# Seven block products for eight in the feed-forward networks, with weights split 1024 columns at a time

## The chip, the core and the metric

One NeuronCore of a Trainium2 chip runs the whole program. The metric is device time in microseconds (us). The kernel before takes 1405.89 us (median of 3 runs, 1405.14 to 1406.78). In what follows PE is TensorE, DVE is VectorE, ACT is ScalarE, POOL is GpSimd and SP is SyncE, which issues most of the transfers.

## The reference

A sequence of 256 rows of width 1024 goes through one block of a first model and two layers of a second. In all there are five feed-forward networks (one in the first block, two in each layer), and between them three mixing stages (attention and recurrence). Everything is float32. A feed-forward network, with `D_FF = 2816`, is

```python
def swiglu(h, w_gate, w_up, w_down):
    return (jax.nn.silu(h @ w_gate) * (h @ w_up)) @ w_down
```

with `h` the normalised rows, `w_gate` and `w_up` of 1024 x 2816 and `w_down` of 2816 x 1024. Around it stand the residual sum and the next norm. The mixing stages multiply by weights of the same height (1024) and do block attention, a gated recurrence or a differential attention on the result.

## The kernel before

**Tiles.** The 256 rows are two tiles `t` of 128. An operand of a matmul is split into a high part (rounded to the type that PE takes at full rate, `fp32r`) and a low part (the rest), and each product is three matmuls, high by high, high by low and low by high (`mm3`). The split of an operand is one copy on ACT (the high part) and one subtraction on DVE (the low part): `split`.

**Weights.** The host lays all weights out as 227 pieces of 128 x 2048 float32 (1 MB). SP loads them in order into three buffers `raw`, and `split_to` splits each piece into two halves of 1024 columns, 512 columns at a time (`SPLIT_W`), into the tiles `wh` (high) and `wl` (low), eight buffers of each (`W_BUFS`). `half` hands one half to the matmuls and splits four halves ahead (`SPLIT_AHEAD`). A half of a gate-and-up piece holds two K blocks of 128 rows by 512 columns; both row tiles use it, so it serves 12 matmuls of 512 columns.

**A feed-forward network** (`ffn_body`) goes over 11 blocks `j` of 256 hidden columns. `gu(t, j)` multiplies the rows of tile `t` by the 512 gate and up columns of block `j` (8 K blocks, 24 matmuls) and makes the hidden values: a Tanh on ACT, two operations on DVE (`th`, `hid`). `turn` transposes the hidden values on PE (4 transposes for both tiles) and splits them (`hh`, `hl`). `dn(t, j)` multiplies them by the 256 rows of `w_down` (12 matmuls) into two PSUM banks that stay open over all blocks. The order is gu(0,j), dn(0,j-1), gu(1,j), dn(1,j-1), so a block is 72 matmuls of 512 columns and 4 transposes.

**The order of work.** PE's order is that of the code (its schedule is manual); transposes and other short work are put into it by `Order`, which keeps a model of PE's time and lets a task go on after a wait written in the code (3.46 in `turn`). ACT, DVE and the transfers are ordered by the scheduler by priority, and `crit()` lifts the work on results over the splits. Each engine works its queue in order. A mixing stage ends with an output projection, for each tile both column halves, after which `boundary` transposes, scales and splits the rows for the next network.

After the sixth block (`j == 5`) some networks call `during`: the first block's network sets up parameters (`second_params`), and in each layer's first network `memory_prep` loads 256 rows of memory, transposes, scales (`uf`) and splits (`mh`, `ml`) them.

## Time and profile before

| | |
|---|---|
| median of 3 runs | 1405.89 us |
| the profiled execution: its own time | 1406.4 us |
| the profiled execution: span of the trace | 1404.6 us |
| busy share of PE, DVE, ACT, POOL | 99%, 66%, 54%, 4% |
| matmuls and transposes on PE | 6598 |
| weights and other data read from HBM | 244.37 MB, 175 GB/s over the span |
| clock granted to PE over the span | 0.999 |

How to read it: the span is cut by the trace into instructions with a start and a duration. Matmuls are pipelined, so the duration of one (about 390 ns) is longer than the distance from its start to the next one's start; it is this distance that counts for a sum. The same holds for DVE and ACT to a smaller degree: in a row of instructions each starts a little before the one ahead has ended. In the rows, `out<-in` names tiles as in the code, `x6` is six instructions, and what stands in brackets is the time that the engine sat idle before and what ended that wait.

### The profile page before, as it was taken

Reading aid. Unit: us, or ns where it says so; the run is one execution under the profiler, and the core shown is the slowest. Engines: PE = TensorE matmul, PEld = TensorE weight load, DVE = VectorE, ACT = ScalarE, POOL = GpSimd, SP = SyncE. Lnnn points to the kernel's source line nnn. Section 1 sums busy time; section 2 is a strip of 40 time slices with the busy share of each in tenths; the row PEclk is TensorE's granted clock in tenths of the full one; section 3 lists DMA queues with packets and bytes.
Section 4 is the critical chain, followed back from the end, with each engine's and each line's share of the span. In section 5 each row is a group of like instructions: output and inputs, shape, how many; then the busy total and the mean of one; then the engine's idle time right before and its main releaser. Section 6 shows DMA issues by size and latency. Waiting matters only on the chain.

```text
span 1404.6 us, 18011 instructions
## 1 busy us (share of the span) xinstructions
PE 1385.3 (99%) x6598; PEld 1126.6 (80%) x6598; DVE 922.8 (66%) x1789; ACT 763.6 (54%) x1527; POOL 58.2 (4%) x59
## 2 busy tenths in 40 slices
PE   8999999999999999999999999999999989999998
PEld 6777888888888888877888888888888767888887
DVE  7866587555585575768576665765756787755554
ACT  6556555444474454668565444644545568544442
POOL 0000000000010000022000000000000121000000
PEclk9999999999999999999999999999999999999999
DMA  8534546555446455454255555555454532455540
GB/s 291 174 122 158 180 142 237 192 191 189 180 157 233 180 180 180 168 197 161 91 183 191 195 187 194 207 191 197 164 206 155 182 120 94 172 188 194 192 180 30
DMA packets 37081, 246.59 MB, mean 176 GB/s; under 512 B 4736, under 2 KB 5760, under 8 KB 8064
## 3 DMA queue, kind: packets, MB, share of 16 engines
q1 hardware_dynamic: 35568, 243.09, 48.2%
q10 hardware_dynamic: 1424, 2.34, 0.5%
q8 instruction: 52, 0.85, 0.2%
q14 instruction: 37, 0.30, 0.1%
HBM read 244.37 MB, written 1.05 MB: 175 GB/s over the span
## 4 chain that ended last, share of the span: by engine, by line
PE 90%; DVE 6%; POOL 2%; ACT 1%; issue 1%; DMA 0%; SPq 0%; DVEq 0%; POOLq 0%; ACTq 0%
PE bank L149 86%; PE trbank L154 4%; POOL fac L261 2%; DVE wl L205 2%; DVE ms L953 1%; ACT p L454 1%; DVE nm L452 1%; DVE z L957 1%; DMA h<-in_x_dram 0%; DVE p L464 0%; DVE p L450 0%; DVE z L1015 0%; DVE p L1052 0%; DVE z L1017 0%; DVE z L1018 0%
## 5 line engine op out<-in xcount | busy, mean ns | idle before, releaser
L205 DVE TENSOR_TENSOR wl<-raw,wh 128x512 fp32r<-128x512 f32 x908 | 580.5, 686 | 194.4 <-ACT wh L204 187.6
L204 ACT CAST wh<-raw 128x512 fp32r<-128x512 f32 x908 | 513.0, 619 | 238.2 <-PE bank L149 227.9
L149 PE MATMUL bank<-wh,uh 128*128 128x512 f32 x1248 | 501.3, 402 | 0.0
L149 PE MATMUL bank<-wl,uh 128*128 128x512 f32 x1248 | 489.5, 392 | 0.0
L149 PE MATMUL bank<-wh,ul 128*128 128x512 f32 x1248 | 489.3, 392 | 0.0
L149 PEld LDWEIGHTS bank<-wh,ul 128*128 128x128 f32 x1248 | 234.6, 188 | 52.6
L149 PEld LDWEIGHTS bank<-wh,uh 128*128 128x128 f32 x1248 | 234.9, 188 | 48.8 <-issue 1.9
L149 PEld LDWEIGHTS bank<-wl,uh 128*128 128x128 f32 x1248 | 235.2, 188 | 46.1 <-DVE wl L205 0.3
L149 PE MATMUL bank<-wh,hh 128*128 128x512 f32 x440 | 172.8, 393 | 0.0
L149 PE MATMUL bank<-wl,hh 128*128 128x512 f32 x440 | 172.0, 391 | 0.0
L149 PE MATMUL bank<-wh,hl 128*128 128x512 f32 x440 | 172.0, 391 | 0.0
L355 ACT ACTIVATE th<-bank,rs 128x256 f32<-128x256 f32 x110 | 52.3, 475 | 179.2 <-PE bank L149 178.4
L356 DVE SCALAR_TENSOR_TENSOR th<-th,bank 128x256 f32<-128x256 f32 x110 | 46.3, 421 | 153.2 <-ACT th L355 153.2
L149 PEld LDWEIGHTS bank<-wl,hh 128*128 128x128 f32 x440 | 82.7, 188 | 18.0
L149 PEld LDWEIGHTS bank<-wh,hl 128*128 128x128 f32 x440 | 82.6, 188 | 17.9
L149 PEld LDWEIGHTS bank<-wh,hh 128*128 128x128 f32 x440 | 82.7, 188 | 17.6
L204 ACT CAST hh<-trbank 128x512 fp32r<-128x512 f32 (+1 forms) x60 | 33.1, 551 | 55.8 <-PE trbank L154 55.8
L261 POOL TENSOR_TENSOR r<-ms,mhalf 128x1 f32<-128x1 f32 x22 | 18.4, 838 | 909.5 <-DVE ms L271 909.5
L358 DVE SCALAR_TENSOR_TENSOR hid<-bank,rs,th 128x256 f32<-128x256 f32 x110 | 53.2, 484 | 3.6
L205 DVE TENSOR_TENSOR hl<-trbank,hh 128x512 fp32r<-128x512 f32 (+1 forms) x60 | 38.8, 646 | 16.5 <-ACT hh L204 13.5
L261 POOL TENSOR_TENSOR fac<-ms,mhalf 128x4 f32<-128x4 f32 (+2 forms) x26 | 38.4, 1477 | 246.8 <-DVE ms L954 139.3
L154 PEld LDWEIGHTS trbank<-cst,hid 128*128 128x128 f32 x220 | 27.6, 140 | 8.1
(223 smaller groups left out, 940.1 us busy)
## 6 DMA issues: line engine op xcount, KB each, us to landing
raw<-in_weights_dram SPq DMA_DIRECT2D x226, 1024.0 KB, 4.9
mem<-in_mem_dram ACTq DMA_DIRECT2D x4, 512.0 KB, 5.5
Tb<-in_rel_dram SPq DMA_DIRECT2D x3, 512.0 KB, 5.8
h<-in_x_dram SPq DMA_DIRECT2D x4, 256.0 KB, 3.8
raw<-in_weights_dram SPq DMA_DIRECT2D x2, 512.0 KB, 7.4
gf<-in_rows_dram SPq DMA_DIRECT2D x1, 512.0 KB, 4.1
out_dram<-h SPq DMA_DIRECT2D x2, 256.0 KB, 2.0
out_dram<-h SPq DMA_DIRECT2D x4, 128.0 KB, 1.8
```

Of the source, the lines that this page charges most:

```text
L149: pe.matmul(out=out, lhsT=lhsT, rhs=rhs, start=start, stop=stop)
L154: pe.transpose(out=out, in_=in_, identity=ident if identity is None else identity)
L204: act.copy(out=hi, in_=src)
L205: dve.tensor_tensor(out=lo, in0=src, in1=hi.bitcast(F32), op=ALU.subtract)
L261: pool.tensor_tensor(out=dst, in0=src, in1=mhalf[:, 0:n], op=ALU.pow)
L355: act.activation(out=th, in_=acc[:, 0:256], func=AF.Tanh, scale=rh[t])
L356: dve.scalar_tensor_tensor(out=th, in0=th, scalar=1.0, in1=acc[:, 0:256], op0=ALU.add, op1=ALU.mult)
L358: dve.scalar_tensor_tensor(out=hd, in0=acc[:, 256:512], scalar=r2[t], in1=th, op0=ALU.mult, op1=ALU.mult)
L452: dve.tensor_reduce(out=nm, in_=s, axis=AX.X, op=ALU.max, negate=True)
L454: act.activation(out=p[:, j, a, 0:n], in_=s[:, j], func=AF.Exp, bias=nm[:, j:j + 1], accum_out=sums[:, j, a:a + 1])
L953: dve.tensor_reduce(out=ms, in_=sq, axis=AX.X, op=ALU.add)
L957: dve.tensor_tensor(out=v, in0=v, in1=fac.unsqueeze(2).to_broadcast([128, n, w]), op=ALU.mult)
```

## The change

In each of the five networks the first seven blocks stay as they were, except that the order of a block is now gu(0,j), gu(1,j), dn(0,j-1), dn(1,j-1). The last four blocks are two groups of two blocks. A group multiplies the rows (2 tiles by 2 halves of K, each 128 x 512 values) by the weights of two blocks (2 halves of K by 2 blocks, each 512 x 512) by Strassen's scheme in the form with 7 products P1 to P7: seven products of 4 K blocks (12 matmuls) in place of eight. The sums of row operands are made once a network (`group_operands`), the sums of weights on DVE from the float32 pieces, 1024 columns at a time (`group_jobs`: `tn`, and in place in `raw` and `rawx`), and the products are joined on DVE (`joined`, tiles `jo`). Each product splits two halves of its own, and such a half serves 6 matmuls. The down products of two earlier blocks stand between the products.

The splits are 1024 columns wide, the buffers `wh` and `wl` are six each, the copies on ACT keep the order of the list of jobs (`in_order`), the output projections go by column half first and tile second, `during` is called after the seventh block, the last before the groups, and the memory rows have one buffer.

```diff
--- before.py
+++ after.py
...
-W_BUFS = 8
+W_BUFS = 6
...
-SPLIT_W = 512
+SPLIT_W = 1024
+GROUPS = 2
...
+    def plain(i):
+        for m in range(2):
+            add_job((i, m), i, lambda i=i, m=m: raws[i][:, 1024 * m:1024 * m + 1024])
...
+            if i in kept:
+                r = kept[i][0].tile([128, 2048], F32, tag="tx", bufs=2, name="rawx")
+            else:
+                r = wp.tile([128, 2048], F32, tag="raw", bufs=RAW_BUFS, name="raw")
...
+    def in_order(inst):
+        if order[0] is not None:
+            tc.add_manual_dep(inst.ins, order[0].ins.name,
+                              mybir.DependencyInfo(mybir.DependencyClass.NoSync, mybir.DependencyReason.DATA),
+                              reason="order of the operands")
+        order[0] = inst
...
+            key, piece, work = jobs[stream["split"]]
+            load_to(piece + 1 + LOAD_AHEAD)
+            r = work()
             hi = wp.tile([128, 1024], FR, tag="wh", bufs=W_BUFS, name="wh")
             lo = wp.tile([128, 1024], FR, tag="wl", bufs=W_BUFS, name="wl")
...
             for s in range(0, 1024, SPLIT_W):
-                split(hi[:, s:s + SPLIT_W], lo[:, s:s + SPLIT_W], r[:, 1024 * m + s:1024 * m + s + SPLIT_W])
-            parts[i, m] = (hi, lo)
+                in_order(split(hi[:, s:s + SPLIT_W], lo[:, s:s + SPLIT_W], r[:, s:s + SPLIT_W]))
+            parts[key] = (hi, lo)
...
-        split_to(2 * i + m + 1 + SPLIT_AHEAD)
+        split_to(at_job[i, m] + 1 + SPLIT_AHEAD)
...
+    def group_jobs(i, pool_, dn):
+        b11, b12, b22, b21 = i, i + 2, i + 3, i + 4
+        kept[b12] = kept[b22] = pool_
+        s = lambda m: slice(1024 * m, 1024 * m + 1024)
+        total = []
+        def job(name, piece, work):
+            for m in range(2):
+                add_job(((i, name), m), piece, lambda m=m: work(m))
+        def add(out, a, b):
+            dve.tensor_tensor(out=out, in0=a, in1=b, op=ALU.add)
+        def t2(m):
+            if m == 0:
+                total.append(pool_[0].tile([128, 2048], F32, tag="tn", bufs=1, name="tn"))
+            add(raws[b11][:, s(m)], raws[b11][:, s(m)], raws[b12][:, s(m)])
+            add(total[0][:, s(m)], raws[b11][:, s(m)], raws[b22][:, s(m)])
+            return total[0][:, s(m)]
+        def t3(m):
+            add(raws[b12][:, s(m)], raws[b12][:, s(m)], raws[b22][:, s(m)])
+            return raws[b12][:, s(m)]
+        def t4(m):
+            add(total[0][:, s(m)], total[0][:, s(m)], raws[b21][:, s(m)])
+            return total[0][:, s(m)]
+        job("P1", b11, lambda m: raws[b11][:, s(m)])
+        plain(dn[0])
+        job("P6", b22, t2)
+        job("P2", b21, lambda m: raws[b21][:, s(m)])
+        job("P5", b21, lambda m: raws[b11][:, s(m)])
+        plain(dn[1])
+        job("P7", b21, t3)
+        job("P3", b21, lambda m: raws[b22][:, s(m)])
+        job("P4", b21, t4)
...
+            full[id(u[2]), k0] = s
...
+        def element(t, j, acc):
+            hid_ready[t, j] = Ready()
             with crit():
                 th = fp.tile([128, 256], F32, tag="th", name="th")
                 act.activation(out=th, in_=acc[:, 0:256], func=AF.Tanh, scale=rh[t])
                 dve.scalar_tensor_tensor(out=th, in0=th, scalar=1.0, in1=acc[:, 0:256], op0=ALU.add, op1=ALU.mult)
-                hd = fp.tile([128, 256], F32, tag="hid", bufs=4, name="hid")
+                hd = fp.tile([128, 256], F32, tag="hid", bufs=5, name="hid")
                 dve.scalar_tensor_tensor(out=hd, in0=acc[:, 256:512], scalar=r2[t], in1=th, op0=ALU.mult, op1=ALU.mult)
-            hids[t] = hd
-            hid_ready[t, j] = ev
-            if j == NJ - 1:
-                side.spawn(turn((t,), j))
-            elif t == 1:
-                side.spawn(turn((0, 1), j))
+            hids[t, j] = hd
...
+        def group_operands():
+            x11, x12, x21, x22 = (full.pop((id(u[t][2]), k)) for t in range(2) for k in (0, 4))
+            sh = fp.tile([128, 4, 4, 128], FR, tag="sh", bufs=1, name="sh")
+            sl = fp.tile([128, 4, 4, 128], FR, tag="sl", bufs=1, name="sl")
+            dve.tensor_tensor(out=x22, in0=x21, in1=x22, op=ALU.subtract)
+            dve.tensor_tensor(out=x21, in0=x11, in1=x21, op=ALU.subtract)
+            dve.tensor_tensor(out=x11, in0=x22, in1=x11, op=ALU.subtract)
+            dve.tensor_tensor(out=x12, in0=x12, in1=x11, op=ALU.add)
+            for n, (name, x) in enumerate((("P6", x11), ("P5", x22), ("P7", x21), ("P3", x12))):
+                split(sh[:, n], sl[:, n], x)
+                S[name] = sh[:, n], sl[:, n]
+            for name, t, k in (("P1", 0, 0), ("P2", 0, 4), ("P4", 1, 4)):
+                S[name] = u[t][0][:, k:k + 4], u[t][1][:, k:k + 4]
...
+        def group(g):
+            j = n_conv + 2 * g
+            a, b = (j - 2, j - 1) if g == 0 else (j - 1, j - 2)
+            last = g == GROUPS - 1
+            i = plan["group", g]
+            def joined(x, y, op, into=None):
+                o = fp.tile([128, 512], F32, tag="jo", bufs=4, name="jo") if into is None else into
+                with crit():
+                    dve.tensor_tensor(out=o, in0=x, in1=y, op=op)
+                return o
+            def prod(name):
+                acc = bank()
+                xh, xl = S[name]
+                for k in range(4):
+                    wh, wl = half((i, name), k // 2, 512)
+                    mm3(acc, xh[:, k], xl[:, k], wh[:, k % 2], wl[:, k % 2], k == 0, k == 3)
+                return acc
+            c11 = fp.tile([128, 512], F32, tag="jo", bufs=4, name="jo")
+            p1_ = prod("P1")
+            with crit():
+                act.copy(out=c11, in_=p1_)
+            dn(1, a)
+            dn(0, a)
+            U = joined(prod("P6"), c11, ALU.add)
+            joined(prod("P2"), c11, ALU.add, c11)
+            element(0, j, c11)
+            if last:
+                side.spawn(turn((0,), j, 4.2))
+            V = joined(prod("P5"), U, ALU.subtract)
+            dn(0, b)
+            p7 = prod("P7")
+            element(1, j + 1, joined(V, p7, ALU.subtract))
+            joined(p7, U, ALU.add, U)
+            if last:
+                side.spawn(turn((1,), j + 1, 4.9))
+            dn(1, b)
+            joined(prod("P3"), V, ALU.add, V)
+            element(0, j + 1, V)
+            side.spawn(turn((0,) if last else (0, 1), j + 1, 4.2))
+            joined(prod("P4"), U, ALU.add, U)
+            element(1, j, U)
+            side.spawn(turn((1,) if last else (0, 1), j, 4.2))
...
+        for j in range(n_conv):
+            more = 1 <= j < n_conv - 1
             gu(0, j)
-            if j:
+            gu(1, j)
+            if more:
                 dn(0, j - 1)
-            gu(1, j)
-            if j:
                 dn(1, j - 1)
-            if during and j == 5:
+            if j == 0:
+                group_operands()
+            if during and j == n_conv - 1:
                 during()
-        j = NJ - 1
-        gu(0, j)
-        dn(0, j - 1)
-        gu(1, j)
-        dn(1, j - 1, (0,))
+        for g in range(GROUPS):
+            group(g)
+        j = NJ - 2
         dn(0, j)
+        dn(1, j + 1, (0,))
+        dn(0, j + 1, by_c=True)
         fin(0)
-        dn(1, j - 1, (1,))
-        dn(1, j)
+        dn(1, j + 1, (1,))
+        dn(1, j, by_c=True)
         fin(1)
...
-        for t in range(2):
-            for c in range(2):
+        for c in range(2):
+            for t in range(2):
                 acc = lin((get_oT(t)[0], get_oT(t)[1], o_ready[t]), (p1 + 2 * c, p1 + 2 * c + 1))
                 sl = h[t][:, 512 * c:512 * c + 512]
                 with crit():
                     dve.tensor_tensor(out=sl, in0=acc, in1=sl, op=ALU.add)
-            res[0].append(boundary(t, h[t], gcol(G_F2 + 8 * layer)))
-            res[1].append(row_rstd(h[t]))
+                if c:
+                    res[0].append(boundary(t, h[t], gcol(G_F2 + 8 * layer)))
+                    res[1].append(row_rstd(h[t]))
...
-            ms = mp.tile([128, 1024], F32, tag="mem", bufs=2, name="mem")
+            ms = mp.tile([128, 1024], F32, tag="mem", bufs=1, name="mem")
```

What the change moves is shown at two places on DVE. The first is the steady work of a network before: one block and a half, where `wl` are splits of weights, `th` and `hid` the hidden values, `hl` the split of the transposed hidden values.

```order
L356 SCALAR_TENSOR_TENSOR th<-th,bank 128x256
L358 SCALAR_TENSOR_TENSOR hid<-bank,rs,th 128x256
L205 TENSOR_TENSOR wl<-raw,wh 128x512 x6
L356 SCALAR_TENSOR_TENSOR th<-th,bank 128x256
L358 SCALAR_TENSOR_TENSOR hid<-bank,rs,th 128x256
L205 TENSOR_TENSOR wl<-raw,wh 128x512 x6
L205 TENSOR_TENSOR hl<-trbank,hh 128x512
```

Now, in the first network, where the first group ends and the second begins; `tn`, `raw` and `rawx` as outputs are sums of weights, `jo` joined products.

```order
L464 SCALAR_TENSOR_TENSOR th<-th,jo 128x256
L267 TENSOR_TENSOR raw<-raw,rawx 128x1024
L466 SCALAR_TENSOR_TENSOR hid<-jo,rs,th 128x256
L223 TENSOR_TENSOR hl<-trbank,hh 128x512
L267 TENSOR_TENSOR tn<-raw,rawx 128x1024
L223 TENSOR_TENSOR hl<-trbank,hh 128x512
L267 TENSOR_TENSOR raw<-raw,rawx 128x1024
L223 TENSOR_TENSOR wl<-tn,wh 128x1024
L267 TENSOR_TENSOR tn<-raw,rawx 128x1024
L267 TENSOR_TENSOR rawx<-rawx 128x1024 x2
L223 TENSOR_TENSOR wl<-tn,wh 128x1024
L223 TENSOR_TENSOR wl<-raw,wh 128x1024 x2
```

Six sums of 1024 columns have come between the splits of weights, and a split waits in DVE's queue behind the sums and joins ahead of it.

The second place is the memory rows of a layer's first network, on DVE; `uf` scales, `ml` is the split. Before they stand between the splits of ordinary blocks:

```order
L356 SCALAR_TENSOR_TENSOR th<-th,bank 128x256
L299 TENSOR_TENSOR uf<-trbank,gc 128x512
L358 SCALAR_TENSOR_TENSOR hid<-bank,rs,th 128x256
L205 TENSOR_TENSOR ml_4470<-uf,mh_4469 128x512
L299 TENSOR_TENSOR uf<-trbank,gc 128x512
L205 TENSOR_TENSOR ml_4470<-uf,mh_4469 128x512
L205 TENSOR_TENSOR wl<-raw,wh 128x512 x6
```

Now they stand inside the first group:

```order
L267 TENSOR_TENSOR rawx<-rawx 128x1024
L371 TENSOR_TENSOR uf<-trbank,gc 128x512
L267 TENSOR_TENSOR tn<-tn,raw 128x1024
L223 TENSOR_TENSOR wl<-raw,wh 128x1024
L223 TENSOR_TENSOR ml_4336<-uf,mh_4335 128x512
L371 TENSOR_TENSOR uf<-trbank,gc 128x512
L223 TENSOR_TENSOR wl<-raw,wh 128x1024
L556 TENSOR_TENSOR jo<-bank,jo 128x512
```

The four scalings and four splits of memory rows moved from blocks where DVE serves 72 matmuls with 12 short splits to a group where sums and joins stand beside them.

## Rows read from the trace of the kernel before

**Rows 1.** The page's busy times: us (share of the span), instructions of each engine.

```profile
PE 1385.3 (99%) x6598; PEld 1126.6 (80%) x6598; DVE 922.8 (66%) x1789; ACT 763.6 (54%) x1527; POOL 58.2 (4%) x59
```

**Rows 2.** Busy time by stretch: two networks, two mixing stages; then PE's clock.

```profile
core 0: us, PE busy (x) PEld busy (x) DVE busy (x) ACT busy (x) POOL busy (x), PEclk, DMA share, GB/s
212.00:400.00 188.00, 188.00 (x847) 153.47 (x846) 115.83 (x208) 93.52 (x172) 3.11 (x3) 1.00 0.54 194
400.00:587.00 187.00, 187.00 (x855) 153.93 (x854) 122.49 (x220) 99.92 (x185) 5.70 (x6) 1.00 0.52 187
587.00:710.00 123.00, 119.97 (x676) 96.00 (x675) 88.08 (x194) 85.51 (x206) 18.32 (x16) 1.00 0.41 145
1083.00:1213.00 130.00, 122.90 (x656) 97.13 (x656) 97.55 (x211) 86.77 (x211) 22.25 (x17) 0.99 0.36 123
```

**Rows 3.** Timeline of PE in a block: start, duration, instruction.

```profile
345.46 0.60 PE L154 MATMUL trbank<-cst,hid 128*128 128x128 f32 x4
345.82 0.48 PE L149 MATMUL bank<-wh,uh 128*128 128x512 f32 x1
...
346.60 0.39 PE L149 MATMUL bank<-wh,uh 128*128 128x512 f32 x1
...
349.34 0.39 PE L149 MATMUL bank<-wh,uh 128*128 128x512 f32 x1
...
350.03 0.40 PE L149 MATMUL bank<-wh,hh 128*128 128x512 f32 x1
...
352.13 0.40 PE L149 MATMUL bank<-wh,hh 128*128 128x512 f32 x1
```

**Rows 4.** Timeline of DVE in a block of the first network.

```profile
303.94 4.01 DVE L205 TENSOR_TENSOR wl<-raw,wh 128x512 fp32r<-128x512 f32 x6 [3.42 <-ACT wh L204]
307.88 0.42 DVE L356 SCALAR_TENSOR_TENSOR th<-th,bank 128x256 f32<-128x256 f32 x1
308.34 0.48 DVE L358 SCALAR_TENSOR_TENSOR hid<-bank,rs,th 128x256 f32<-128x256 f32 x1
308.74 3.69 DVE L205 TENSOR_TENSOR wl<-raw,wh 128x512 fp32r<-128x512 f32 x6
```

**Rows 5.** Groups of DVE by shape: count, busy us, mean ns, idle before.

```profile
L205 DVE TENSOR_TENSOR wl<-raw,wh 128x512 fp32r<-128x512 f32 x908 | 580.5, 686 | 194.4 <-ACT wh L204 187.6
L1269 DVE TENSOR_TENSOR h<-h,gf 128x1024 f32<-128x1024 f32 x2 | 2.4, 1219 | 0.0
L402 DVE SCALAR_TENSOR_TENSOR h<-bank,h 128x512 f32<-128x512 f32 x18 | 12.3, 687 | 2.2 <-PE bank L149 2.0
L205 DVE TENSOR_TENSOR hl<-trbank,hh 128x256 fp32r<-128x256 f32 x10 | 4.2, 419 | 3.3 <-ACT hh L204 3.3
L205 DVE TENSOR_TENSOR ml<-uf,mh 128x512 fp32r<-128x512 f32 x8 | 5.5, 692 | 2.1 <-ACT mh L204 2.0
```

**Rows 6.** Groups of ACT by shape.

```profile
L204 ACT CAST wh<-raw 128x512 fp32r<-128x512 f32 x908 | 513.0, 619 | 238.2 <-PE bank L149 227.9 <-DMA raw<-in_weights_dram 5.2 <-ACT wh L204 2.8
L355 ACT ACTIVATE th<-bank,rs 128x256 f32<-128x256 f32 x110 | 52.3, 475 | 179.2 <-PE bank L149 178.4 <-DVE hl L205 0.7
L267 ACT ACTIVATE junk<-h 128x1024 f32<-128x1024 f32 x18 | 19.0, 1058 | 24.7 <-DVE h L1197 19.8 <-DMA h<-in_x_dram 2.9 <-DVE h L402 1.5
```

**Rows 7.** The transfers of weights: KB each, median us from issue to landing.

```profile
raw<-in_weights_dram SPq DMA_DIRECT2D x226, 1024.0 KB, 4.9
```

**Rows 8.** Waits of PE: us in total, times, longest.

```profile
PE trbank L154 <- DVE z L1018: 3.3, 2, 2.3
PE trbank L154 <- DVE p L1052: 2.2, 1, 2.2
PE trbank L154 <- DVE o L957: 1.6, 3, 0.8
```

**Rows 9.** Timeline of PE in the last mixing stage; idle before in brackets.

```profile
1129.50 0.66 PE L154 MATMUL trbank<-cst,p 128*128 128x128 f32 x2 [2.18 <-DVE p L1052]
```

**Rows 10.** The stretch in which PE's clock fell (columns as in rows 2).

```profile
1128.90:1132.30 3.40, 2.80 (x8) 2.33 (x9) 3.40 (x8) 2.24 (x7) 0.00 (x0) 0.50 0.21 34
```

More of the change, by code (lines that the diff above doesn't have):

```diff
@@ L188, with add_job @@
     stream = {"load": 0, "split": 0}
-    raws, parts = {}, {}
+    raws, parts, kept = {}, {}, {}
     NP = weights.shape[0]
+    jobs, at_job = [], {}
+    piece_at = {}
+    def add_job(key, piece, work):
+        at_job[key] = len(jobs)
+        jobs.append((key, piece, work))
+    def plain(i):
+        for m in range(2):
+            add_job((i, m), i, lambda i=i, m=m: raws[i][:, 1024 * m:1024 * m + 1024])
     def load_to(n):
@@ L203, in split @@
     def split(hi, lo, src):
-        act.copy(out=hi, in_=src)
+        c = act.copy(out=hi, in_=src)
         dve.tensor_tensor(out=lo, in0=src, in1=hi.bitcast(F32), op=ALU.subtract)
+        return c
+    order = [None]
+    def in_order(inst):
[4 more added lines that the diff above has]
+        order[0] = inst
     def split_to(n):
-        while stream["split"] < min(n, 2 * NP):
-            i, m = divmod(stream["split"], 2)
-            load_to(i + 1 + LOAD_AHEAD)
-            r = raws[i]
+        while stream["split"] < min(n, len(jobs)):
+            key, piece, work = jobs[stream["split"]]
+            load_to(piece + 1 + LOAD_AHEAD)
+            r = work()
             hi = wp.tile([128, 1024], FR, tag="wh", bufs=W_BUFS, name="wh")
@@ L287, in new_u @@
         return uh, ul, []
+    full = {}
     def put_T(u, k0, n, src, gains=None, gain1=None, keep=None):
@@ L390, in dn @@
             hh, hl = hidT[t, j]
-            order = [(c, k) for c in range(2) for k in kts] if j == NJ - 1 else [(c, k) for k in kts for c in range(2)]
-            for c, k in order:
-                wh, wl = half(dnp(j), k, 512)
-                mm3(accd[t][c], hh[:, k], hl[:, k], wh[:, c], wl[:, c], j == 0 and k == 0, j == NJ - 1 and k == 1)
+            done[t] += len(kts)
+            order = [(c, k) for c in range(2) for k in kts] if by_c else [(c, k) for k in kts for c in range(2)]
+            for n, (c, k) in enumerate(order):
+                wh, wl = half(plan["dn", j], k, 512)
+                first = (t, c) not in started
+                started.add((t, c))
+                mm3(accd[t][c], hh[:, k], hl[:, k], wh[:, c], wl[:, c], first,
+                    done[t] == 2 * NJ and (c, k) == [o for o in order if o[0] == c][-1])
+        done = [0, 0]
         def fin(t):
@@ L407, in fin @@
                 finish(t)
-        for j in range(NJ - 1):
+        S = {}
+        def group_operands():
[11 more added lines that the diff above has]
+                S[name] = u[t][0][:, k:k + 4], u[t][1][:, k:k + 4]
@@ L422, in ffn_body @@
-        dn(1, j - 1, (0,))
+        for g in range(GROUPS):
+            group(g)
+        j = NJ - 2
         dn(0, j)
+        dn(1, j + 1, (0,))
+        dn(0, j + 1, by_c=True)
         fin(0)
-        dn(1, j - 1, (1,))
-        dn(1, j)
+        dn(1, j + 1, (1,))
+        dn(1, j, by_c=True)
         fin(1)
@@ L1191, in second_mix @@
         res = [[], []]
-        for t in range(2):
-            for c in range(2):
+        for c in range(2):
+            for t in range(2):
                 acc = lin((get_oT(t)[0], get_oT(t)[1], o_ready[t]), (p1 + 2 * c, p1 + 2 * c + 1))
@@ L1245, in memory_kv, with plan_ffn @@
             side.spawn(task())
-    P_FFN = 3 * NJ
+    plans = {}
+    for n in range(30):
+        plain(n)
+    p = 30
+    def plan_ffn():
+        nonlocal p
+        plans[p] = ffn_plan(p)
+        p += P_FFN
+    plan_ffn()
+    for layer in range(2):
+        plan_ffn()
+        for n in range(16):
+            plain(p + n)
+        p += 16
+        plan_ffn()
+    assert p == NP
     p = 0
```

88 lines of the change are left out of this document (64 added, 24 removed).

## The prediction

> **What bounds the kernel now.** I read the page's busy times first: PE is busy 1385.3 us of the span of 1404.6, and DVE 66% of it [rows 1]. The table by stretch says where PE is not busy: in the two networks that it shows PE is busy 188.00 of 188.00 and 187.00 of 187.00 us, and the idle time lies in the mixing stages, 3.0 us (123.00 less 119.97) and 7.1 us (130.00 less 122.90) [rows 2]. So a network costs what its matmuls cost, as long as DVE and ACT bring the split weights in time; DVE is busy 115.83 of the 188 us [rows 2]. The timeline gives the price of a matmul. From 346.60 to 349.34 us twelve matmuls on row operands start, 0.228 us each; from 350.03 to 352.13 nine on hidden values, 0.233 each; four transposes take 0.36, or 0.09 each [rows 3].
>
> **What the change removes.** A group has 7 x 12 = 84 product matmuls where two blocks had 4 x 24 = 96, and the 48 down matmuls stay. Ten groups save 120 matmuls, 120 x 0.228 = 27.4 us. All of it lay on the path, since PE never paused there.
>
> The Trainium skill's page "TensorE: Matmul & The Clock Gate", section "Back-to-back issue gap", puts a matmul of 512 columns in a stream with its weight loads at about 131 ns. By that the 120 would save 15.7 us and the sum below would end 12 us higher. The trace differs, with 228 ns from start to start [rows 3], so the sum goes by it and the rule gets no chance of its own.
>
> **What it adds on DVE.** First the prices. Six splits of 512 columns take 3.69 us and one takes 0.686, so they start 0.60 apart, 0.09 less than one lasts [rows 4, 5]. An operation on 1024 columns lasts 1.219 us [rows 5]; with the same overlap of 0.09 it occupies DVE for 1.13. No row shows 1024 columns back to back. The bounds are 1.22 (no overlap) and 1.07 (twice the 0.533 us by which 1024 exceeds 512, so without any fixed cost). I take 1.13, since the overlap is what rows 4 show. A join of a product in PSUM costs what a residual sum from PSUM does, 0.687, so 0.60 in a row [rows 5]. `th` and `hid` last 0.42 and 0.48 [rows 4], so 0.33 and 0.40 in a row, a 256-column `hl` 0.33 [rows 5]. The copy of 1024 columns on ACT lies between 0.619 for 512 columns and 1.058 for a Square of 1024 [rows 6]; I take 1.05.
>
> In an ordinary block this is no burden: 6 splits at 1.13 in place of 12 at 0.60 (6.8 for 7.2 us), with 72 matmuls and 4 transposes, 16.9 us, to hide under. In a group it is. There are 14 splits for products, 4 for down weights and 8 sums, 26 x 1.13 = 29.4 us, then 7 joins, 4 pairs of `th` and `hid` and the `hl`, 4.2 + 2.9 + 1.2: 37.7 us of DVE against 132 matmuls and 8 transposes, 31.1 us of PE. ACT has 18 x 1.05 + 4 x 0.475 and about 2 us of other copies, 23 us [rows 6], and stays under PE.
>
> What can be done ahead is limited by the six buffers. The first group profits: its first splits and sums run while gu(0,6) and gu(1,6) still multiply, and I price its waits at nothing (DVE has the last conventional block's idle time as cover; gone, the group would wait the 6.6 us of its excess). The second does not. Its splits stand in DVE's queue behind the last two splits of group one (P4), and the first of these needs the buffer of the first half of P7. From the end of that half of P7 I count both queues up to the second half of P4 in group two, which PE needs there.
>
> - PE: 168 matmuls (108 on rows, 60 on hidden values) and 12 transposes: 108 x 0.228 + 60 x 0.233 + 12 x 0.09 = 39.7 us.
> - DVE, by its order from the split of P4 to that second half: 20 splits and 8 sums of 1024 columns, 28 x 1.13 = 31.7; 10 joins, 6.0; 5 `th` and 5 `hid`, 3.7; 2 `hl` of 512 and 2 of 256 columns, 1.9: 43.3 us. Ahead of it stand the end of the matmul (0.39 less 0.23 [rows 3], 0.16) and the copy on ACT, 1.05, behind it the last split's own end, 0.09: 44.6 us.
>
> PE waits for the difference, 4.9 us a network, 24.5 us in five. With 1.07 it is 3.2, with 1.22 it is 7.4 a network: 16 to 37.
>
> **What stands behind it.** DVE is then still late. The two down splits that follow cost 1.5 and 2.1 us (each with a `th`, a `hid` or a join in front) while PE takes 1.37 and 1.40 for a half: 0.8 us. The last hidden tile passes a join, a Tanh (0.475 [rows 6]), `th`, `hid`, two transposes and a split on each engine, 3 us, but on DVE behind splits for the next network, and the first rows of the next network come from the same queue. PE has 8.4 us of down products to cover this. I take 2.0 us a network for all this, 10 us in five; bounds 0.8 and 4.
>
> - The memory rows add 8 operations of 0.60 [rows 5], 4.8 us, to group one of two networks. They lay in ordinary blocks; now DVE has about 2 us to spare ahead of P4. 3 us each, 6 us; bounds 0 and 9.6.
> - `group_operands` adds 4 sums and 4 subtractions of 512 columns, 4.8 us, in the first blocks, where DVE is idle 6.6 us a block ((188.00 less 115.83) / 11 [rows 2]). Its cover holds except where the new network's rows are late too: 1 us a network, 5 us; bounds 0 and 24.
> - Mixing stages: PE waits there for chains of short operations on DVE and ACT [rows 8]. A chain's operation can stand behind a split that lasts 1.22 in place of 0.69 on DVE and 1.05 in place of 0.62 on ACT. DVE is 75% busy there (97.55 of 130 [rows 2]), so a handover loses about 0.2 us (half of the 0.53 that the split lasts longer, in 75% of the cases); six waits with four handovers each in the last stage make 5 us, and I take nothing for the other two. The new order of the output projection also asks for the second tile's attention result 24 matmuls (5.5 us) earlier. I take these 5 us; bounds -3 (the new order also takes a split's wait away) and 14.
> - Transfers: a group loads 6 pieces in 31 us, a block 3 in 16.9. A piece lands 4.9 us after its issue [rows 7], and the buffers that it waits for come free more than 8 us of DVE work before it is needed: nothing; if one were late, up to 4.9 us a group.
>
> **Sum.** -27.4 + 24.5 + 10 + 6 + 5 + 5 = +23 us on the profiled execution's 1406.4, or 1429.5. The median shown is 0.5 us below that execution: 1429.
>
> **Rivals.**
>
> - The clock falls too, 1441 us. In the last mixing stage PE waited 2.18 us after light work [rows 9] and its clock was 0.50 of full, 1.2 GHz, for 3.4 us [rows 10], which cost half of them, 1.7 us. If the waits of each second group and two more in the last mixing stage do the same, 7 x 1.7 = 12 us come on top. Against it: another wait of 2.3 us [rows 8] stands in the same stage, whose mean clock of 0.99 [rows 2] is one fall's worth, and in a group dense matmuls lie between waits of 1 to 2 us. The skill's page "TensorE: Matmul & The Clock Gate", section "HAM oscillation", warns of just such kernels, in which pauses that recur bring the slow clock each time; rows 10 agree that it happens.
> - Faster, 1389 us: DVE keeps up. It is one mechanism: the queue of the second group fits under PE's 39.7 us. It decides at 0.96 us for an operation on 1024 columns (28 x 0.17 = 4.9 us less). Then the waits, the tail and the memory rows' price vanish, and -27.4 + 5 + 5 remain. For it speak DVE's 34% of idle time [rows 1] and its 194.4 us of waiting ahead of splits [rows 5]; against it the row of 1.219 us and that the buffers forbid using the idle time of other blocks.
> - In between, 1403 us: the wait of the second group comes as counted (24.5), but all the rest is hidden. The mixing stages would have to keep their waits, which are already there with shorter splits.
>
> That the saving does not come is not a rival: the order has 120 matmuls fewer on PE.
>
> **Chances.** The forecast 0.71, the slower clock 0.14, DVE keeping up 0.08, the case between 0.07. A measurement of this kernel tells about 0.2% (2.8 us) from no change. The case between falls on either side of that bound: 0.03 faster, 0.04 the same. So faster 0.11, the same 0.04, slower 0.85. The range goes from 1411, where the run costs 1.07 and the small terms half of theirs (-27.4 + 16 + 5 + 3 + 3 + 5, about +5), to 1446, where it costs 1.22 (+12) and the mixing stages 5 more.
>
> **What would show it.** Right: in the second group of each network PE's waits are on `wl`, DVE shows no gap for about 43 us there, its 1024-wide splits start 1.13 apart, the first group of the first network has no wait, and a network takes some 2 us longer than before (5 in the two with memory rows), not 5.5 shorter. Wrong: PE without waits in the groups, or splits of 1.0 us; PE waiting for transfers; a clock of 0.5 in the groups.

## The result, and the profile after

The changed kernel takes 1437.65 us (median of 4 runs, 1436.41 to 1437.94), the kernel before 1405.78 beside it: ratio 1.0224, with a 95% interval of 1.0207 to 1.0242. It is slower, by 31.9 us where 23 were forecast, and lies inside the range.

The page of the profiled execution (its own time 1436.41 us) answers to [rows 1] and [rows 5]: the span, busy time by engine, the head of the chain that ended last, and the split on DVE.

```profile
span 1434.6 us, 17202 instructions
PE 1376.8 (96%) x6478; PEld 1100.2 (77%) x6478; DVE 1106.8 (77%) x1590; ACT 797.0 (56%) x1168; POOL 65.3 (5%) x59
PE 72%; DVE 20%; ACT 3%; issue 2%; POOL 2%; DMA 1%; DVEq 0%; POOLq 0%; ACTq 0%
L223 DVE TENSOR_TENSOR wl<-raw,wh 128x1024 fp32r<-128x1024 f32 x434 | 526.0, 1221 | 134.2 <-ACT wh L222 125.7
```

PE has 120 matmuls and transposes fewer (6478 for 6598) and is busy 8.5 us less, but the span is 30.0 us longer, and a fifth of the chain now runs over DVE (6% before). A split of 1024 columns lasts 1.221 us, the 1.219 that the sum's price was made from.

Cut at the networks' first and last matmuls, the tables by stretch (columns as in [rows 2]) show where the 30 us are. First the kernel after: network 1, the gap behind it, network 2, the first and the last mixing stage between networks.

```profile
213.24:404.20 190.96, 186.23 (x829) 149.13 (x827) 154.81 (x188) 102.07 (x126) 3.22 (x2) 1.00 0.49 171
404.20:406.36 2.16, 0.17 (x1) 0.00 (x1) 2.12 (x6) 2.16 (x5) 0.00 (x0) 1.00 0.92 372
406.36:603.10 196.74, 190.20 (x845) 152.09 (x846) 160.89 (x206) 109.29 (x140) 4.84 (x5) 0.99 0.51 178
603.10:724.07 120.97, 116.30 (x653) 92.13 (x652) 82.92 (x156) 79.86 (x168) 19.30 (x16) 1.00 0.42 152
1110.36:1242.77 132.41, 120.69 (x635) 94.06 (x634) 93.50 (x174) 81.47 (x174) 22.75 (x17) 0.99 0.38 135
```

And the kernel before, networks 1 and 2 and the same two mixing stages.

```profile
212.65:402.18 189.53, 189.53 (x854) 154.67 (x853) 117.36 (x208) 95.25 (x176) 4.06 (x3) 1.00 0.53 191
402.18:591.81 189.63, 189.63 (x870) 156.22 (x868) 124.35 (x226) 102.18 (x190) 5.19 (x6) 1.00 0.53 189
591.81:710.47 118.66, 115.63 (x654) 92.36 (x653) 84.51 (x187) 81.52 (x199) 17.39 (x15) 1.00 0.41 144
1087.89:1214.02 126.13, 119.03 (x636) 93.92 (x634) 94.44 (x205) 82.72 (x204) 21.32 (x16) 0.99 0.36 123
```

The five networks, cut in this way, take +1.4, +7.1, +2.7, +6.2 and +1.3 us: 18.7 us more, where 27.4 us of matmuls are gone. The gap is new, 2.2 us; the two mixing stages are 2.3 and 6.3 us longer; the start is 0.6 longer. That is 30.1.

Inside the networks the table by stretch shows the first and the second group of network 1, then of network 2, where the memory rows are made.

```profile
321.69:352.78 31.09, 31.09 (x137) 25.18 (x136) 29.71 (x35) 20.59 (x23) 0.00 (x0) 1.00 0.55 203
352.78:389.56 36.78, 33.38 (x145) 25.52 (x144) 36.46 (x44) 20.62 (x26) 0.00 (x0) 1.00 0.33 114
516.24:549.30 33.06, 32.75 (x153) 26.66 (x152) 32.38 (x42) 21.49 (x28) 1.73 (x1) 1.00 0.61 205
549.30:588.46 39.16, 33.81 (x145) 25.50 (x144) 38.61 (x46) 21.13 (x28) 0.00 (x0) 1.00 0.31 105
```

The first group takes 31.09 us and PE never pauses. In the second DVE is busy 36.46 of 36.78 us and PE pauses: it is idle 3.4 us of the 5.7 by which this group is longer than the first; the rest the trace doesn't show as idle time. DVE's timeline there has the columns of [rows 4]; of the run from the split of P4 in group one to that in group two it shows the start, two operations in a row, and the end.

```profile
344.31 1.23 DVE L223 TENSOR_TENSOR wl<-tn,wh 128x1024 fp32r<-128x1024 f32 x1 [1.11 <-ACT wh L222]
...
360.45 1.22 DVE L223 TENSOR_TENSOR wl<-tn,wh 128x1024 fp32r<-128x1024 f32 x1
361.59 1.22 DVE L267 TENSOR_TENSOR tn<-raw,rawx 128x1024 f32<-128x1024 f32 x1
...
387.04 1.22 DVE L223 TENSOR_TENSOR wl<-tn,wh 128x1024 fp32r<-128x1024 f32 x1
```

From 344.31 to the end of the last, 388.26, are 43.95 us, where 43.3 were counted, with starts 1.13 to 1.14 apart. PE's waits, which answer to [rows 8], are led by the tile that DVE writes (us in total, times, longest; `bank` is the output of a matmul, `trbank` that of a transpose):

```profile
PE bank L152 <- DVE wl L223: 20.4, 31, 1.8
...
PE trbank L157 <- DVE cc L1236: 3.8, 1, 3.8
...
PE bank L152 <- ACT uh L222: 2.0, 1, 2.0
```

The clock shows one fall more than before, and not in a group: behind the gap of network 1, where PE had waited 2.0 us for `uh`. The table by stretch, ahead of it and in it:

```profile
404.20:407.60 3.40, 1.41 (x5) 0.76 (x5) 3.36 (x8) 3.40 (x6) 0.42 (x1) 1.00 0.95 388
407.60:411.05 3.45, 3.45 (x12) 2.79 (x12) 1.78 (x7) 2.26 (x4) 1.59 (x2) 0.51 1.01 420
```

### The profile page after: what moved, and what is told of

Read it like the earlier page. It is cut to its first block, busy times and chain, and to the rows that moved or that the text cites. A ratio compares the mean times of both kernels' runs of the same rounds, so it can differ in the third digit from the quotient of the medians.

```text
span 1434.6 us, 17202 instructions
## 1 busy us (share of the span) xinstructions
PE 1376.8 (96%) x6478; PEld 1100.2 (77%) x6478; DVE 1106.8 (77%) x1590; ACT 797.0 (56%) x1168; POOL 65.3 (5%) x59
## 4 chain that ended last, share of the span: by engine, by line
PE 72%; DVE 20%; ACT 3%; issue 2%; POOL 2%; DMA 1%; DVEq 0%; POOLq 0%; ACTq 0%
PE bank L152 69%; DVE wl L223 9%; PE trbank L157 4%; DVE jo L556 2%; POOL fac L330 2%; DVE tn L267 2%; ACT wh L222 1%; ACT p L640 1%; DVE raw L267 1%; DVE hl L223 1%; DVE hid L466 1%; DVE nm L638 1%; DVE th L464 1%; DVE rawx L267 1%; DVE ms L1140 1%
## 5 line engine op out<-in xcount | busy, mean ns | idle before, releaser
L223 DVE TENSOR_TENSOR wl<-raw,wh 128x1024 fp32r<-128x1024 f32 x434 | 526.0, 1221 | 134.2 <-ACT wh L222 125.7
L222 ACT CAST wh<-raw 128x1024 fp32r<-128x1024 f32 x434 | 449.8, 1049 | 202.0 <-PE bank L152 184.7
L152 PE MATMUL bank<-wh,uh 128*128 128x512 f32 x1048 | 418.7, 399 | 2.0 <-ACT uh L222 2.0
L152 PE MATMUL bank<-wl,uh 128*128 128x512 f32 x1048 | 412.1, 393 | 4.0 <-DVE wl L223 4.0
L152 PE MATMUL bank<-wh,ul 128*128 128x512 f32 x1048 | 412.7, 394 | 0.1
L152 PEld LDWEIGHTS bank<-wl,uh 128*128 128x128 f32 x1048 | 197.6, 189 | 49.5 <-DVE wl L223 8.8
L152 PE MATMUL bank<-wl,sh 128*128 128x512 f32 x160 | 63.7, 398 | 11.1 <-DVE wl L223 11.1
L222 ACT CAST wh<-tn 128x1024 fp32r<-128x1024 f32 x40 | 42.1, 1051 | 47.8 <-DVE tn L267 35.2
L152 PE MATMUL bank<-wh,sh 128*128 128x512 f32 x160 | 63.8, 399 | 0.7 <-ACT wh L222 0.7
L152 PE MATMUL bank<-wh,sl 128*128 128x512 f32 x160 | 62.7, 392 | 0.0
```

The costliest lines, as they stand in the source:

```text
L152: pe.matmul(out=out, lhsT=lhsT, rhs=rhs, start=start, stop=stop)
L222: c = act.copy(out=hi, in_=src)
L223: dve.tensor_tensor(out=lo, in0=src, in1=hi.bitcast(F32), op=ALU.subtract)
```

## The experiments

The theory under test is the queue theory: in the second group VectorE has more to do than TensorE, and that is what the change pays for. Its rivals are that loads and buffers make PE wait (the sums would not matter), and that splits of twice the width and six buffers cost by themselves, wherever they stand.

### No groups, one group

`e1_g0`, all else in the code as after (the list of weight pieces and the call of `group_operands` follow). One thing moves with it: `during` follows the last block ahead of the groups, so without groups the memory rows are made behind the eleventh block, at the network's end.

```diff
-GROUPS = 2
+GROUPS = 0
```

> All eleven blocks of a network go the conventional way; the 1024-wide splits, the six buffers and the new order of the output projection stay. Queue theory (VectorE has more to do in the second group than TensorE, and that is what the change pays for): the networks come back to the 187 to 190 us that they took before, and only the mixing stages keep what they grew by, 9.2 us; about 1416 us. Width theory (1024-wide splits and six buffers cost by themselves, wherever they stand): ordinary blocks wait too, and 1425 us or more.

Measured: 1432.43 us (1428.88 to 1433.95), ratio to before 1.0192 (1.0175 to 1.0209). The queue theory's 1416 is a miss. The networks are nearly back (190.60 us for the first), but the first and last mixing stages take more than in the changed kernel itself:

```profile
212.53:403.13 190.60, 189.91 (x853) 154.55 (x852) 113.27 (x137) 89.86 (x109) 3.23 (x2) 1.00 0.53 182
593.84:720.49 126.65, 119.05 (x662) 93.85 (x660) 86.66 (x162) 81.75 (x172) 17.26 (x16) 0.99 0.41 145
1099.82:1235.25 135.43, 123.04 (x643) 95.68 (x642) 96.78 (x180) 83.26 (x177) 20.60 (x17) 0.97 0.36 125
```

Part of that is the memory rows. The first mixing stage, which begins at 593.84, now holds half of their transposes, and PE waits in it for their `uf` (in the last mixing stage too, 2.1 us), as it does in no kernel with groups:

```profile
594.52 0.60 PE L157 MATMUL trbank<-cst,mem 128*128 128x128 f32 x4
PE trbank L157 <- DVE uf L371: 2.1, 1, 2.1
```

So what surrounds the groups costs 26 us where a network ends in ordinary blocks and in the memory rows, and the groups in their place add 5 to that. A kernel without groups that makes the memory rows early was not run, so how much of the 26 us is their place stays open.

`e2_g1`:

```diff
-GROUPS = 2
+GROUPS = 1
```

> One group in each network in place of two. Queue theory: a lone group is a first group, which waited for nothing (31.09 us in the first network); the 33.7 us by which the five second groups exceed 31.1 us go, and 60 matmuls x 0.228 = 13.7 us of saving go with them: 1437.7 - 33.7 + 13.7, about 1418 us, if nothing but the second group is late. If the tail behind the last group is its own cost, it stays in that. Width theory: half of what the groups cost stays, 1425 us or more.

Measured: 1414.79 us (1413.39 to 1415.33), ratio 1.0062 (1.0047 to 1.0077): 23 us less than with two, where 20 were expected. The lone group of the first network by stretch:

```profile
355.88:387.42 31.54, 31.54 (x141) 25.54 (x140) 30.17 (x36) 21.85 (x26) 0.00 (x0) 1.00 0.40 141
```

It stands last in its network and PE is busy 31.54 of 31.54 us. That a group is the last is not what makes it late; that one stands ahead of it is.

### Less and more work on VectorE

`e10_nosum` keeps of the eight sums the two that `t2` makes last:

```diff
-            add(raws[b11][:, s(m)], raws[b11][:, s(m)], raws[b12][:, s(m)])
-            add(raws[b12][:, s(m)], raws[b12][:, s(m)], raws[b22][:, s(m)])
-            add(total[0][:, s(m)], total[0][:, s(m)], raws[b21][:, s(m)])
```

> Six of the eight sums of weights of each group are left out, so that three of its seven products are made of other weights than they should be. Queue theory: 6 x 1.13 = 6.8 us leave VectorE's 43.3 us of the second group, which is more than its excess of 5.7 to 8.1 us in most networks; the waits of the second group and the 2 us in the first groups of the second and fourth network go, 33.7 + 4 us, about 1400 us; the mixing stages keep their 9 us. Latency theory (loads and buffers, not the sums): over 1430 us.

Measured: 1405.51 us (1403.45 to 1406.47), ratio 0.9996 (0.9987 to 1.0005): 32.1 us less than with the sums, where 37.7 were expected. The second groups of networks 1 and 2:

```profile
352.82:385.77 32.95, 32.18 (x146) 25.91 (x144) 31.71 (x39) 23.29 (x28) 0.00 (x0) 1.00 0.38 134
544.19:576.57 32.38, 31.60 (x145) 25.90 (x144) 32.02 (x40) 23.08 (x28) 0.00 (x0) 1.00 0.37 131
```

They shrink by 3.8 and 6.8 us and keep 1.9 over the 31.1 and 30.5 of a group without waits. Loads, buffers and order are as they were, so the latency theory falls: it wanted over 1430.

`e4_twice` makes each sum twice:

```diff
             dve.tensor_tensor(out=out, in0=a, in1=b, op=ALU.add)
+            dve.tensor_tensor(out=out, in0=a, in1=b, op=ALU.add)
```

> Each of the eight sums of weights of a group is made twice on VectorE (two of the sums are made in place, so what is computed differs). Queue theory: 9.0 us more in each of ten groups, less the 2 to 3 us that VectorE has left in a first group: 75 to 90 us more, 1513 to 1528 us. Latency theory: the second sum delays a half once, not the queue: under 20 us more, under 1458 us.

Measured: 1549.89 us in one run, 112 us more, where the queue theory wanted 75 to 90. The 80 added sums of 1.13 us come to 90.4, but not each is paid where it stands: the first group of network 1 takes 36.74 us, 5.6 more for 9.0 of added sums. The clock is lower too: the mean over the run, and the second group of network 1 by stretch (the granted clock is the third column from the end).

```profile
core 0: 1548.1 us, clock 0.967
358.46:408.83 50.37, 38.35 (x145) 28.15 (x144) 47.94 (x54) 21.83 (x28) 0.00 (x0) 0.90 0.25 84
```

A mean of 0.967 is about 100 us at 1.2 GHz, where the changed kernel has two falls of 3.4 us. With waits that add up to so much the clock falls inside the groups too, as it did not in the changed kernel. How the 112 us divide over the sums and the clock was not separated, so the run shows that work on VectorE is paid for, and not at what price.

### The sums on GpSimd

`e3_pool`:

```diff
-            dve.tensor_tensor(out=out, in0=a, in1=b, op=ALU.add)
+            pool.tensor_tensor(out=out, in0=a, in1=b, op=ALU.add)
```

> The eight sums of weights of each group are made by GpSimd in place of VectorE; nothing else is changed. Queue theory: 8 x 1.13 = 9.0 us leave VectorE's 37.7 us of a group, so it stays under TensorE's 31.1 us; the waits of both groups go (33.7 us in the second, 4 us in the first), about 1400 us, provided that GpSimd makes a sum in well under 3.9 us (31.1 / 8) and that VectorE isn't slowed beside it. Latency theory (TensorE waits because a half can be loaded and split only when one of six buffers is free, whatever the sums cost): no change, 1438 us, or slower by what a sum takes longer.

Measured: 1533.87 us (1533.53 to 1534.43), ratio 1.0911 (1.0894 to 1.0927). GpSimd made a sum in 2.8 to 3.2 us on average, under the 3.9, but the other condition failed. Its timeline in the first network, and then DVE's over the same time:

```profile
319.65 3.39 POOL L267 TENSOR_TENSOR raw<-raw,rawx 128x1024 f32<-128x1024 f32 x1
323.11 3.26 POOL L267 TENSOR_TENSOR tn<-raw,rawx 128x1024 f32<-128x1024 f32 x1
...
360.89 3.24 POOL L267 TENSOR_TENSOR tn<-raw,rawx 128x1024 f32<-128x1024 f32 x1
...
367.38 3.32 POOL L267 TENSOR_TENSOR rawx<-rawx 128x1024 f32<-128x1024 f32 x1
```

```profile
320.69 3.43 DVE L223 TENSOR_TENSOR wl<-raw,wh 128x1024 fp32r<-128x1024 f32 x1
324.04 3.41 DVE L223 TENSOR_TENSOR wl<-tn,wh 128x1024 fp32r<-128x1024 f32 x1
...
361.82 0.68 DVE L556 TENSOR_TENSOR jo<-bank,jo 128x512 f32<-128x512 f32 x1
...
368.43 2.56 DVE L464 SCALAR_TENSOR_TENSOR th<-th,jo 128x256 f32<-128x256 f32 x1
```

The sum that starts at 319.65 ends at 323.04; the split that starts beside it, at 320.69, ends at 324.12, 1.08 us later, which is about what a split takes alone. The next pair ends at 326.37 and 327.45, again 1.08 apart: the two take turns. Two splits start 3.35 us apart where 1.13 was the rule, so a sum on GpSimd takes up to 2.2 us from DVE, up to 8 x 2.2 = 18 us a group in place of the 9.0 that it was to free. The last two rows show which operations suffer: the join at 361.82, with one input in PSUM, lies inside a sum and lasts 0.68 us as ever, while `th` at 368.43, with both inputs in SBUF, lasts 2.56 us in place of 0.42. The run thus says nothing against the queue theory; it loads the same queue more. How much of its 96 us more than the changed kernel is this, and how much that GpSimd's sums come late, was not separated. The Trainium skill's page "SBUF — State Buffer", section "SBUF: two separate sides", says that a VectorE operation with two SBUF inputs and a GpSimd operation that reads SBUF lock each other out for a whole instruction. These two timelines agree: the 1.1 us of a split and the 2.2 for which the sum keeps it waiting make the 3.35 between two starts.

### The memory rows

`e7_early`:

```diff
-            if during and j == n_conv - 1:
+            if during and j == 2:
```

> The memory rows are made in the third block of their network, in place of the last block ahead of the groups. Queue theory: their 4.8 us of VectorE fall where it has idle time; the first groups of the second and fourth network shrink from 33.06 to 31.1 us and the second groups from 39.15 to 36.8, 2 x 4.3 us less, about 1429 us. If memory rows cost by their transposes and matmuls wherever they stand, no change, 1438 us.

Measured: 1430.61 us (1430.29 to 1431.51), 7.0 us less than after. The two groups of network 2:

```profile
516.70:547.20 30.50, 30.50 (x137) 25.18 (x136) 29.50 (x35) 20.54 (x23) 0.00 (x0) 1.00 0.57 207
547.20:584.08 36.88, 33.21 (x145) 25.52 (x144) 36.60 (x45) 20.68 (x26) 0.00 (x0) 1.00 0.33 114
```

They are 2.6 and 2.3 us shorter and now like those of network 1: the memory rows' place ahead of the groups was their price.

### What surrounds the groups

Three kernels without groups take the surroundings apart; in all three the memory rows stand at the network's end, as in `e1_g0`. `e5_g0_512` has the narrow splits, `e6_g0_512_8` eight buffers as well, `e13_g0_proj` the old order of the output projections besides (the same edit in both mixing stages):

```diff
 GROUPS = 0
-SPLIT_W = 1024
+SPLIT_W = 512
```

```diff
-W_BUFS = 6
+W_BUFS = 8
```

```diff
-            for c in range(2):
-                for t in range(2):
+            for t in range(2):
+                for c in range(2):
                     acc = lin(mT[t], (p2 + 2 * c, p2 + 2 * c + 1))
```

> As the kernel without groups (1432.4 us), but the weights are split in two pieces of 512 columns again; six buffers and the new order stay. Width theory (a chain's operation stands behind a split of 1.22 us in place of 0.69): the mixing stages, 126.6 and 135.4 us without groups, come back to the 118.7 and 126.1 of before, and the time to about 1410 us. Buffer theory (six buffers in place of eight let less be split ahead) or order theory (the new order of the output projection and of the last two down blocks): they stay, about 1430 us.

> As the run before, with eight buffers as well: only the order of the output projection and of the last two down blocks differs from the kernel before. Order theory: as long as with six buffers, 1425 us or more. Buffer theory: about 1410 us here, and not with six. Width theory: about 1408 us in both.

> As the kernel without groups with 512-wide splits and eight buffers (1414.9 us), and the output projections go by row tile first again, as in the kernel before. Order theory of the mixing stages: they come back from 120.3 and 130.4 us to 118.7 and 126.1, and the time to about 1409 us; the rest, some 4 us, lies in the order of the blocks in the networks (188.0 to 190.6 us for 186.9 to 189.6). If it isn't the projection, 1415 us.

Measured: 1431.17 (1426.02 to 1432.98), 1414.93 (1414.87 to 1417.81) and 1415.94 us (1412.56 to 1416.34). The width does nothing that can be told: 1.0188 (1.0171 to 1.0205) against 1.0192 with wide splits. Six buffers cost 16 us here (8 between the two profiled executions), and the memory rows have a part in it: with six PE waits 3.6 us in all for their `uf` at the head of the two mixing stages, with eight not at all. The order of the projections does nothing either, 1.0068 (1.0055 to 1.0080) against 1.0073 (1.0058 to 1.0088). The two mixing stages of the third kernel (120.29 and 130.36 us in the second):

```profile
593.96:714.11 120.15, 116.81 (x661) 92.94 (x660) 86.96 (x192) 82.87 (x201) 19.87 (x16) 1.00 0.40 142
1093.08:1222.27 129.19, 119.50 (x644) 93.53 (x643) 98.61 (x213) 85.57 (x209) 23.74 (x17) 1.00 0.35 120
```

With narrow splits, eight buffers and the old projections the mixing stages still are 1.5 and 3.1 us longer than before, and the whole 10 us. Eight transposes of the memory rows (0.60 us for four) are in each of the two stages. What is left of the edit (the order of the blocks, the copies on ACT kept in the order of the jobs, the single buffer of the memory rows and their place at the network's end) was not taken apart.

### The groups kept apart

`e11_apart` puts a conventional block between the two groups; six lead in place of seven (the list of weight pieces follows):

```diff
-        n_conv = NJ - 2 * GROUPS
+        n_conv = 6
...
-            a, b = (j - 2, j - 1) if g == 0 else (j - 1, j - 2)
+            j, a, b = ((6, 4, 5), (9, 6, 8))[g]
...
-        for g in range(GROUPS):
-            group(g)
+        group(0)
+        gu(0, 8)
+        gu(1, 8)
+        dn(0, 7)
+        dn(1, 7)
+        group(1)
```

> Both groups stay, with all their sums, splits and six buffers; one conventional block moves from ahead of the first group to between the two. Queue theory: each group then has a block ahead of it in which VectorE is idle 6.4 us (16.9 us of TensorE, 10.5 of VectorE), about its excess of 6.6; the 33.7 us by which the second groups exceed 31.1 us go, but for what six buffers keep from being done ahead: 1404 to 1412 us. Theory that any group ahead of the down products of the end is late (the last group's chain of join, Tanh, transposes): no more than 10 us less, 1428 us or more.

Measured: 1409.14 us (1407.55 to 1411.02), ratio to before 1.0027 (1.0016 to 1.0039): 28.5 us less than the changed kernel, with the same matmuls, sums and splits. The first network by stretch: first group, block, second group; then the second group of network 2.

```profile
304.66:335.75 31.09, 31.09 (x137) 25.18 (x136) 29.71 (x35) 21.21 (x24) 0.00 (x0) 1.00 0.59 208
335.75:354.09 18.34, 18.16 (x85) 14.68 (x84) 16.37 (x22) 9.01 (x12) 0.00 (x0) 1.00 0.50 178
354.09:385.20 31.11, 31.11 (x138) 25.14 (x136) 29.63 (x35) 19.48 (x24) 0.00 (x0) 1.00 0.35 127
546.50:577.00 30.50, 30.50 (x137) 25.12 (x136) 29.53 (x35) 19.26 (x24) 0.00 (x0) 1.00 0.36 131
```

PE no longer pauses in any second group: 31.11 us for 36.78, and 30.50 for 39.16. In the block between, which has idle time on DVE, its busy time is 16.37 of 18.34 us: the excess is carried into it. This settles the question between the theories of the second group, with no work taken away.

`e12_apart_early` has the edit of `e7_early` as well:

> As the run before, and the memory rows are made in the third block of their network. Queue theory: they stood ahead of the first group still, so 2 to 4 us in each of two networks go: 4 to 8 us less than the run before, about 1400 us, and less than the kernel before the change (1405.7). If the first group has room enough for them there, no difference.

Measured: 1406.46 us (1403.75 to 1408.91), ratio 1.0007 (0.9998 to 1.0015): 2.7 us less, not 4 to 8, and no faster than before. In network 4 PE waits 2.0 us for the `hid` of the first block, whose place on DVE is beside `group_operands` (1.6 us in the run before), and its clock falls behind that. The stages say why it is no faster: the first mixing stage takes 120.97 us, as in the changed kernel, and the last this:

```profile
1084.49:1217.95 133.46, 123.28 (x635) 95.80 (x634) 93.53 (x174) 81.43 (x173) 22.73 (x17) 0.96 0.38 134
```

Against the profile before, the span is 0.3 us longer, the start 0.7 and the two mixing stages 2.3 and 7.3; so the networks are 10.0 us shorter, and the mixing stages take it back.

`e14_three`, from the run before:

```diff
-GROUPS = 2
+GROUPS = 3
...
-        n_conv = 6
+        n_conv = 3
...
-            if during and j == 2:
+            if during and j == 1:
...
-            j, a, b = ((6, 4, 5), (9, 6, 8))[g]
+            j, a, b = ((3, 1, 2), (6, 3, 5), (9, 6, 8))[g]
```

> A version that might beat the kernel before: three groups in each network, each with a conventional block straight ahead of it (three blocks, a group, a block, a group, a block, a group), and the memory rows in the second block. Queue theory: 60 more matmuls x 0.228 = 13.7 us go; VectorE, busy 153.9 of 186.1 us in the first network with two groups kept apart, gets 37.7 - 2 x 10.5 = 16.7 us more, 170.6 of 183.4, so it still fits as a whole; but a block and a group together take 48.2 us of VectorE and 48.0 of TensorE, so nothing is left to catch up with, and some of the saving goes in waits: 1406.5 - 13.7 and 3 to 8 us back, 1396 to 1401 us. If six buffers can't carry over that much, the waits eat all of it: 1406 us or more.

Measured: 1404.57 us (1400.54 to 1410.69), ratio to before 0.9990 (0.9978 to 1.0003). It is the fastest, but not by more than the measurement can tell, and the forecast of 1396 to 1401 is a miss. The groups themselves hold, but for the first of networks 2 and 4 (32.07 and 32.06 us), which follow the memory rows; the second group and the second block between of network 1, and that block in network 4, by stretch, with PE's waits in the last:

```profile
303.44:334.11 30.67, 30.67 (x134) 24.80 (x133) 29.07 (x33) 18.88 (x23) 0.00 (x0) 1.00 0.54 197
334.11:352.55 18.44, 18.18 (x86) 14.68 (x84) 18.14 (x23) 10.27 (x13) 0.00 (x0) 1.00 0.56 183
1018.10:1040.60 22.50, 19.86 (x85) 15.85 (x84) 18.29 (x23) 10.35 (x14) 0.00 (x0) 0.92 0.47 149
```

```profile
PE trbank L157 <- DVE hid L462: 2.6, 1, 2.6
```

In the second block DVE is busy 18.14 of 18.44 us: nothing is left to catch up with. In network 4 PE waits 2.6 us for `hid` there and its clock falls; in network 2, which is in the same order, that block takes 18.5 us, and why the two differ stays open. Of the 13.7 us the profiled run kept none: its span is 1405.1 us, and 1404.9 in the run before. How the loss divides over the other small waits was not worked out.

## Why the prediction was right

**The saving and the second group.** The sum's two largest terms hold. The matmuls went, and DVE's run in the second group measured 43.95 us for 43.3. Against the same groups kept apart, where PE never pauses, the five second groups are 5.7, 8.7, 6.4, 8.6 and 6.4 us longer (36.78 less 31.11, 39.16 less 30.50, and so on). That is 35.7 us. The tails behind them add 1.8. The first groups of networks 2 and 4 with the memory rows add 2 x 2.5. Together that is 42.6, and the forecast for the queue, the tail and the memory rows was 24.5 + 10 + 6 = 40.5. With the saving, the gap, the stretches up to the first groups, the mixing stages and the start, some 2 of the 30.1 us are left unexplained. Inside, the sizes shift: the queue costs 5.7 to 6.4 us where it stands alone (4.9 forecast), the tail inside a network 0.4 more than with the groups apart, where PE still waits 0.9 in it (2.0 forecast), and the new gap behind network 1 adds 2.2 once. The memory rows cost 7.0 us by `e7_early`, where 6 were forecast.

**Operands.** `group_operands` was given 5 us. The stretch up to the first group grows by 1.1 and 0.6 us in networks 2 and 4 (in network 2 the slow clock's 1.7 us lie in it) and not at all in the others: its cover, DVE's idle time in the first blocks, held.

**Mixing stages.** They cost 8.6 us where 5 were forecast, and the step given for them is borne out only in part: "A chain's operation can stand behind a split that lasts 1.22 in place of 0.69". The trace has such a place. In the last mixing stage PE waits 3.8 us, 2.3 at the most before, while on DVE a split of weights stands between two operations of the chain on `z`:

```profile
1156.22 1.22 DVE L223 TENSOR_TENSOR wl<-raw,wh 128x1024 fp32r<-128x1024 f32 x1
...
1157.44 0.66 DVE L1205 TENSOR_TENSOR z<-z,z 128x512 f32<-128x512 f32 x1
```

But narrow splits give back only 1 us, within the error, in the kernel without groups and with six buffers; with groups, or with eight buffers, the width was not run. The projections' new order, which the prediction named beside the splits, is not it. The two stages take 121.0 and 132.3 to 133.5 us wherever the groups stand and whether there are one, two or three of them, so the groups are not their price either. Without groups and with six buffers they are longer still (126.65 and 135.43 us), and there PE's waits for the memory rows' `uf` are new. What makes up the 8.6 us stays open, and that a forecast of 5 came as near is partly luck.

**The rivals.** The clock fell once more than before, 1.7 us, not seven times, and at a network's boundary; `e4_twice` shows that the rival's mechanism is real once the waits grow. DVE did not keep up: an operation on 1024 columns took 1.22 us, 1.13 in a row, where 0.96 was the point of decision. The case between needed a free tail and unchanged mixing stages, and had neither.

**What the sum did not show.** A total that comes out near hides that the groups need not lose. Kept apart, with all their sums, splits and six buffers, the kernel takes 23.3 us less than the one without groups (1432.43 less 1409.14). Not all of that is the saving of matmuls. Between the two profiled executions the span differs by 20.8 us; the mixing stages, which have no group in them, are 7.9 us shorter (120.98 and 133.19 for 126.65 and 135.43) and the start 0.7 longer, so the networks save 13.6 of the 27.4 us of their matmuls. And the surroundings without any group, the memory rows' place among them, cost 26.4.

## What to carry to other kernels

Where an engine at 66% has to feed a bound one at 99%, count its queue over the stretch that the buffers can bridge, not over the span: two heavy stretches side by side cost 28.5 us here that one light stretch between them gave back. An algorithm that saves matmuls and adds elementwise work is paid for in buffers as well, so time its surroundings (width, buffers, order) with the algorithm switched off before giving the loss to the algorithm, and look at what else the switch moves: here it moved the memory rows to the network's end. A second elementwise engine is relief only if its operation and the first one's don't exclude each other: here a sum on GpSimd took up to 2.2 us from VectorE, where making it there costs 1.13.

## What the hardware showed that was not expected

- A VectorE split (both inputs in SBUF) beside a GpSimd sum of 3.3 to 3.4 us lasts 3.41 to 3.43 us in place of 1.22. A join, with one input in PSUM, is spared: ten of them overlap a sum in `e3_pool`, and none lasts over 0.69 us.
- A wait of 2.0 us at a network's boundary was followed by 3.4 us at 1.2 GHz, while waits of up to 1.8 us in the second groups, with dense matmuls around them, were not.
